# A hybrid decoder layer: four edits to where sums land, when loads are issued and how the order of the work is reckoned

## The chip, the cores and the metric

The kernel runs on one core of a Trainium2 chip. The metric is the device time of the whole program in microseconds (us), the median of several executions. The engines are called PE (TensorE), DVE (VectorE), ACT (ScalarE), POOL (GpSimd) and SP (SyncE, which here only issues transfers).

## The reference

One decoder layer in float32 on x of 1024 positions by 1024 channels. Cut to what is computed:

```python
h = rms_norm(x, ln_pre_mix)
proj = h @ w_in                      # 256 pooling channels, then q, k, v of 12 heads of 64
u, q, k, v = split(proj)
pool = multi_scale_pool(u, ...)      # 4 groups of 64: trailing means over 2/4/8/16 positions,
                                     # minus the token, a 64x64 map, a scale per channel
for window, dilation in ((128, 1), (512, 4), (2048, 16)):
    o, lse = dilated_branch(rope(q), rope(k), v, window, dilation)
o = sum(softmax(lse over the three) * o)
mixed = concat(pool, o)
x1 = x + rms_norm(mixed @ w_out, ln_post_mix)
g = rms_norm(x1, ln_pre_ffn)
f = (silu(g @ w_gate) * (g @ w_up)) @ w_down       # D_FF = 2816
out = x1 + rms_norm(f, ln_post_ffn)
```

## The kernel before, in words

**Numbers.** Every float32 operand of a large product is split into two float32r parts, a rounded one (hi, a cast on ACT) and what is left (lo, a subtraction on DVE or POOL). A product is three passes over them: hi by hi, hi by lo, lo by hi. `split` (L147 to 152) does both halves for a weight tile `wraw`; `wtile` loads and splits one. Channels lie on partitions, positions on the free axis, in two halves h of 512 positions.

**Attention stage (to about 410 us).** There are twelve units, a pair of heads p and a half h each. A unit has `scores` (products into banks `ps_s`, the mask and running minimum on DVE at L528, the exponential on ACT at L531), `merge` (the softmax joining: small DVE sums `ex`, a small PE product `ps_o<-ex,ls`, at L545), `weigh` (the probabilities `pp` multiplied by `wv` on POOL and DVE, L581) and `values` (turns of `pp` into `ps_t`, then products with v). Each step has a position in `plan`, a number given in the table `PRM`; `emit` sorts the steps by position and writes the program in that order. PE keeps program order; on DVE, ACT, POOL and SP a scheduler sets the order from modelled times.

The input projection's products (`ps_pj`) are the Fill between the steps. Besides having positions of their own, they are pulled by a reckoned clock: `clock` grows with every step written (0.235 per Fill product, 0.47 per score step), `due[key]` says at which reckoned time a result should be there, and `await_(key)` writes Fill products until the clock has come to it, at most 12 at a time. Table entries that matter below: `ls` (what follows a score step), `lw` (the weights of the joining), `f0` (where a unit's Fill starts), `first` (positions of unit 0), `cm` (splits of the mixed features).

**Pooling** is in unit 0 to 1: `pool_proj` makes `uf` and its split `u` (L692 to L695), `pool_means` multiplies u by band matrices (`ps_o<-band,u`), `pool_product` maps (`ps_o<-dhl,wp`).

**Output projection.** `mixed` loads the mixed features back (`mraw`) and splits them (`m`, L860/L861). `out_proj(h)` runs eight output tiles d; tile d's weights come by `weights(d)`, which is called at the middle of tile d-1, into `wraw` (two buffers). For h=1, tiles d=3 and d=5 have a split tile of their own, the others share `whl`. `chain(h)` is the norm after it, the residual sum with a second load of x (`xr`), the store `x1d` and the norm before the feed-forward part.

**Feed-forward.** The first two f tiles are plain products (`gate_up`). Then come ten groups j, in which a 2 by 2 block product is done with seven products P1 to P7 (`seven`), each as two rows i of 12 matmuls. `taken` and `gated` add the seven up on DVE: P1 is kept in `q` and `sq`, P7 in `sq` and `p`, and P5's bank `ps_s` is added to P7's. `down_sums` makes block sums of the down weights on POOL beside it. The last stage, from 988 us, is the down product, again by seven products; `operands` casts them on ACT and takes their lo parts on POOL (L1343) and DVE (L1344). The weights of the first group's seven (`rw`, L1193) are loaded and cast early, by `ahead`.

Nearly all transfers are issued by SP, in its order; one that has to wait for a buffer holds up those behind it.

Of the kernel before, what the change touches and what calls it, by code (L numbers as in the profile page):

```python
# [15 lines left out]
P = 128  # L16
# [54 lines left out]

# [36 lines left out]
def hybrid_block(ctx: ExitStack, tc: tile.TileContext, xT, w_in, w_pin, w_pool, w_out, w_gate, w_up, w_down,  # L108
# [28 lines left out]

    def raw_tile(src):
        r = wpool.tile([P, 1024], F32, name="wraw", tag="wraw", bufs=2)
        if len(src.ap) == 2:  # L140
            nc.sync.dma_start(r, src)
            return r
        r = r[:, :src.shape[1] * P]
        nc.sync.dma_start(r.rearrange("p (k m) -> p k m", m=P), src)
        return r
# [7 lines left out]

    def wtile(src, eng=None, pool=None, tag="whl", bufs=2):
        r = raw_tile(src)
        w = (pool or wpool).tile([P, 2, 1024], F32R, name=tag, tag=tag, bufs=bufs)
        split(w[:, :, :r.shape[-1]], r, eng or nc.gpsimd)
        return w
# [195 lines left out]
    def need(key, n):  # L354
        assert seen.get(key, 0) >= n, (key, n, seen.get(key, 0))
# [64 lines left out]
    G = PRM  # L420
# [64 lines left out]
    def scores(pr, h):  # L485
# [5 lines left out]
        def step(hd, side, jj):  # L491
# [26 lines left out]
            clock[0] += 0.47  # L518
            due["s", 0], due["s", 1] = due.get(("s", 1), 0.0), clock[0] + G["ls"]
            for j in (2 * jj, 2 * jj + 1):  # L520
                nb = 1 if narrow(side, h, j) else 2
                lo = 256 - nb * P
                so = s[:, (j % 2) * 256:(j % 2) * 256 + nb * P]
                row, mask = pt[:, j, lo:], (mB if side else mA)[:, lo:]
                if side == 0:
                    so = by_class(so)
                    row, mask = (x.rearrange("p (r c) -> p r c", c=4) for x in (row, mask))
                nc.vector.tensor_tensor_reduce(  # L528
                    row, so, mask, op0=ALU.add, op1=ALU.min, scale=-0.125,
                    scalar=3e38, accum_out=sx[:, 0, side, j, hd, 0:1])  # L530
                nc.scalar.activation(pt[:, j, lo:], pt[:, j, lo:], AF.Exp,  # L531
                                     bias=sx[:, 0, side, j, hd, 0:1], scale=-1.0,
                                     accum_out=sx[:, 0, side, j, hd, 1:2])
        return [lambda a=a: step(*a) for a in [(hd, sd, jj) for hd in range(2) for sd in (1, 0) for jj in range(2)]]

    def merge(pr, h):

        need(("s", pr.p, h), 8)
        un = pr.un[h]
        sx = un.sx  # L540
# [137 lines left out]
    def pool_proj(tt, k, n):  # L678
# [7 lines left out]
        if k == NK - 1 and n == 2:  # L686
# [7 lines left out]
            nc.scalar.activation(hi, f, AF.Copy)  # L694
            nc.gpsimd.tensor_tensor(lo, f, hi.bitcast(F32), ALU.subtract)  # L695

    def pool_bands():
# [6 lines left out]
    def pool_means(i, h):  # L704

        did(("means", i, h))
        d = pool.w["d", i, h] = att.tile([P, 2, 512], F32R, name="dhl", tag="ptr", bufs=PTB)
        sl = slice(i * P, (i + 1) * P)
# [124 lines left out]
    for u in range(1, 11):  # L833
        put(Fill([x for f in fill[u] for x in f]).by(3), u + G["f0"], u + (0.25 if u == 10 else 1) + G["f1"])
    put(Fill([x for h in range(2) for x in v_half(pairs[0], h)]).by(3), 0.0, G["pw"])
# [11 lines left out]
    def mixed(h, raw):  # L847
# [10 lines left out]
        def cut(n, sl):  # L858
            m[h][n] = room(h, n)
            nc.scalar.activation(m[h][n][:, sl, 0], got[n], AF.Copy)  # L860
            nc.vector.tensor_tensor(m[h][n][:, sl, 1], got[n], m[h][n][:, sl, 0].bitcast(F32), ALU.subtract)  # L861
        ids = [(n, slice(0, 1 if n == 2 else 2)) for n in (0, 1, 3, 2)]
# [22 lines left out]
    def out_proj(h, parts, done):  # L885
# [3 lines left out]
        def weights(d):  # L889
            if d not in box:  # L890
                box[d] = wtile(w_out[d], nc.gpsimd if d < 2 else nc.vector,
                               *((xgp, "xk5", 1) if d == 2 else (ffnl, "b%d" % (4 + d // 4), 1) if h and d in (3, 5) else ()))

# [34 lines left out]
    lm, cm = mixed(0, raws((0, 1)))  # L928
    put(lm, G["lm"], G["lm"])
    for step, at in zip(cm + [near], G["cm"]):  # L930
        put([step], at, 0)
    st, weights = out_proj(0, 3, None)
    put([lambda f=weights: f(0)], G["lm"], 0)
    put([lambda f=weights: f(1)], G["cm"][2], 0)
# [72 lines left out]
    def chain(h, sq, s3, at):  # L1007
# [4 lines left out]
        def load():  # L1012
            for n in range(2):
                x.append(slot((6, 4)[h] + n, [P, 4, 512], F32, "xr%d" % n))
                nc.sync.dma_start(x[n], xT[:, 4 * n:4 * n + 4, sl])

# [43 lines left out]

    emit((out_proj(1, 3, sqs[1][0].add)[0], 0.0, 1.0), *chain(0, *sqs[0], G["c0"]))

# [97 lines left out]
    def seven(j, order, rooms=()):  # L1160
# [66 lines left out]
        def taken(p, i):  # L1227
# [13 lines left out]
            elif p != "P5" or ("P7", i) in t:  # L1241
                own = [t[{"P4": "P1", "P5": "P7", "P3": "P6"}[p], n] for n in range(i + 1)]

                sum_to = own[i] if p == "P5" else ps
                nc.vector.tensor_tensor(sum_to, own[i], ps, ALU.add)
# [26 lines left out]
    one, ahead = seven(EARLY // 2, ("P1", "P2", "P6", "P5", "P7", "P4", "P3"), (6, 7))  # L1272
    ahead = ahead()
    ws += [{0: ftile(w_gate[f], f), 1: ftile(w_up[f], f)} for f in range(1, EARLY)]
# [271 lines left out]
```

## Time and profile before

| | |
|---|---|
| runs | 1214.27, 1218.79, 1220.18 us; median 1218.79 |
| profiled execution | 1218.72 us, of which the span is 1216.9 |
| PE busy | 1160.3 us, 95% of the span |
| DVE, POOL, ACT busy | 805.2 (66%), 596.3 (49%), 541.1 (44%) |
| transfers | 158.6 MB, mean 130 GB/s |
| PE idle from 561 to 984 us | none to speak of |

A busy time is the union of an engine's instructions. A number in brackets behind a row of the timeline is idle time of that engine just before, with the instruction that the profile names as its end. The column of PE's clock is the granted share of full speed: 1.00 is 2.4 GHz, and 0.50 would be 1.2 GHz, so 0.86 over a stretch of 25 us means that 7 us of it (0.14 / 0.5 x 25) were at the lower level.

### The profile page before, as it was taken

Reading aid. Unit: us, or ns where it says so; the run is one execution under the profiler, and the core shown is the slowest. Engines: PE = TensorE matmul, PEld = TensorE weight load, DVE = VectorE, ACT = ScalarE, POOL = GpSimd, SP = SyncE. Lnnn points to the kernel's source line nnn. Section 1 sums busy time; section 2 is a strip of 40 time slices with the busy share of each in tenths; the row PEclk is TensorE's granted clock in tenths of the full one; section 3 lists DMA queues with packets and bytes.
Section 4 is the critical chain, followed back from the end, with each engine's and each line's share of the span. In section 5 each row is a group of like instructions: output and inputs, shape, how many; then the busy total and the mean of one; then the engine's idle time right before and its main releaser. Section 6 shows DMA issues by size and latency. Waiting matters only on the chain.

```text
span 1216.9 us, 16713 instructions
## 1 busy us (share of the span) xinstructions
PE 1160.3 (95%) x5942; PEld 980.2 (81%) x5942; DVE 805.2 (66%) x1465; ACT 541.1 (44%) x1021; POOL 596.3 (49%) x533
## 2 busy tenths in 40 slices
PE   8999999999999898899999999999999989999996
PEld 6888888878887787777888888888888868888896
DVE  7935967686868756667965756566565584454585
ACT  6455655553656665475532232223321435343430
POOL 0131536364345222232176787577765967656521
PEclk9998999999999899999999999999999999999998
DMA  7101101011101312842034443554444849666642
GB/s 267 56 22 53 44 27 44 27 32 38 44 27 53 105 70 87 287 146 96 18 142 187 156 180 140 185 196 165 156 158 169 280 161 383 215 208 190 191 138 70
DMA packets 68435, 158.60 MB, mean 130 GB/s; under 512 B 8064, under 2 KB 11392, under 8 KB 66944
## 3 DMA queue, kind: packets, MB, share of 16 engines
q1 hardware_dynamic: 67776, 157.01, 37.1%
q8 instruction: 47, 0.77, 0.3%
q10 hardware_dynamic: 576, 0.52, 0.1%
q14 instruction: 36, 0.29, 0.1%
HBM read 114.51 MB, written 42.99 MB: 129 GB/s over the span
## 4 chain that ended last, share of the span: by engine, by line
PE 78%; DVE 13%; issue 3%; POOL 2%; DMA 2%; ACT 2%; SPq 0%; DVEq 0%; POOLq 0%; ACTq 0%
PE ps_pj L113 28%; PE ps_o L113 21%; PE ps_s L113 20%; PE ps_t L113 6%; PE ps_t L116 3%; DVE pp L528 1%; DVE sq L1209 1%; DMA mraw<-mixd 1%; DVE ql L344 1%; DVE k L337 1%; DVE rsw L312 1%; DVE ptr L622 1%; DVE whl L152 1%; DVE b L1022 1%; DVE v L478 1%
## 5 line engine op out<-in xcount | busy, mean ns | idle before, releaser
L113 PE MATMUL ps_pj<-x,whl 128*128 128x512 f32 x720 | 215.8, 421 | 1.5 <-ACT whl L148 0.9
L113 PEld LDWEIGHTS ps_pj<-x,whl 128*128 128x128 f32 x720 | 131.4, 193 | 19.6 <-ACT whl L148 1.1
L1203 POOL TENSOR_TENSOR fw<-rw,fw 128x512 fp32r<-128x512 f32 x74 | 106.3, 1460 | 61.5 <-ACT fw L1201 61.4
L581 POOL TENSOR_SCALAR pp<-pp,wv 128x256 f32<-128x256 f32 (+1 forms) x156 | 72.6, 484 | 95.8 <-DVE wv L565 91.9
L113 PE MATMUL ps_o<-tT,fw 128*128 128x512 f32 x504 | 117.8, 390 | 0.0
L531 ACT ACTIVATE pp<-pp,sx 128x128 f32<-128x128 f32 (+1 forms) x192 | 89.5, 467 | 54.7 <-DVE sx L528 54.1
L113 PEld LDWEIGHTS ps_o<-tT,fw 128*128 128x128 f32 x504 | 94.6, 188 | 20.0
L1203 POOL TENSOR_TENSOR whl<-rw,whl 128x512 fp32r<-128x512 f32 x42 | 61.5, 1488 | 58.6 <-ACT whl L1201 58.6
L314 POOL TENSOR_TENSOR rsw<-rsw,sinr 128x512 f32<-128x512 f32 x20 | 26.2, 1308 | 116.4 <-DVE rsw L312 116.4
L1201 ACT ACTIVATE fw<-rw 128x1024 fp32r<-128x1024 f32 x37 | 38.5, 1056 | 95.9 <-DVE rw L1169 40.9
L1343 POOL TENSOR_TENSOR op<-rw,op 128x512 fp32r<-128x512 f32 x38 | 60.7, 1596 | 39.3 <-ACT op L1342 37.3
L152 POOL TENSOR_TENSOR whl<-wraw,whl 128x512 fp32r<-128x512 f32 x34 | 46.0, 1374 | 59.4 <-ACT whl L148 59.4
L1342 ACT ACTIVATE op<-rw 128x1024 fp32r<-128x1024 f32 x38 | 40.3, 1061 | 64.6 <-PE ps_t L113 34.2
L622 DVE TENSOR_TENSOR ptr<-ps_t,ptr 128x512 fp32r<-128x512 f32 (+1 forms) x84 | 56.0, 668 | 16.5 <-ACT ptr L621 15.8
L621 ACT ACTIVATE ptr<-ps_t 128x512 fp32r<-128x512 f32 (+1 forms) x84 | 48.3, 576 | 41.6 <-PE ps_t L116 37.5
L113 PE MATMUL ps_pj<-b,fw 128*128 128x512 f32 x264 | 62.3, 392 | 0.0
L113 PE MATMUL ps_o<-ptr,v 128*128 128x128 f32 (+1 forms) x472 | 58.6, 259 | 3.8 <-DVE ptr L622 3.8
L113 PE MATMUL ps_s<-k,qh 128*128 128x128 f32 (+1 forms) x192 | 54.7, 296 | 6.4 <-DVE sx L528 6.3
L113 PEld LDWEIGHTS ps_o<-ptr,v 128*128 128x128 f32 x472 | 52.8, 165 | 7.4 <-DVE ptr L622 4.4
L113 PEld LDWEIGHTS ps_pj<-b,fw 128*128 128x128 f32 x264 | 49.6, 188 | 10.9
L113 PEld LDWEIGHTS ps_s<-k,qh 128*128 128x128 f32 x192 | 48.8, 254 | 11.7 <-DVE sx L528 8.4
L113 PE MATMUL ps_o<-tT,whl 128*128 128x512 f32 x216 | 52.3, 397 | 0.0
(302 smaller groups left out, 2898.6 us busy)
## 6 DMA issues: line engine op xcount, KB each, us to landing
rw<-bd SPq DMA_DIRECT2D x77, 256.0 KB, 4.6
rw<-wsd SPq DMA_DIRECT2D x44, 256.0 KB, 3.9
rw<-in_w_gate_dram SPq DMA_DIRECT2D x20, 512.0 KB, 3.6
rw<-in_w_up_dram SPq DMA_DIRECT2D x20, 512.0 KB, 4.6
wraw<-in_w_in_dram SPq DMA_DIRECT2D x17, 512.0 KB, 3.5
bd<-p SPq DMA_DIRECT2D x33, 256.0 KB, 2.9
rw<-in_w_down_dram SPq DMA_DIRECT2D x33, 256.0 KB, 4.9
wraw<-in_w_out_dram SPq DMA_DIRECT2D x16, 512.0 KB, 3.9
```

The lines of the kernel that those rows point to most:

```text
L113: return tc.keep_in_program_order(nc.tensor.matmul(*a, **k))
L116: return tc.keep_in_program_order(nc.tensor.transpose(dst, src, by))
L152: eng.tensor_tensor(dst[:, 1, at:at + w], src[:, at:at + w], dst[:, 0, at:at + w].bitcast(F32), ALU.subtract)
L314: eng[0].tensor_tensor(s, s, sinr[:, sl], ALU.mult)
L531: nc.scalar.activation(pt[:, j, lo:], pt[:, j, lo:], AF.Exp, bias=sx[:, 0, side, j, hd, 0:1], scale=-1.0, accum_out=sx[:, 0, side, j, hd, ...
L581: nc.gpsimd.tensor_scalar(pv, pv, un.wv[:, side, j, hd:hd + 1], 1.0, op0=ALU.mult, op1=ALU.mult)
L621: nc.scalar.activation(ptr[:, 0, :w], t[:, :w], AF.Copy)
L622: nc.vector.tensor_tensor(ptr[:, 1, :w], t[:, :w], ptr[:, 0, :w].bitcast(F32), ALU.subtract)
L1201: nc.scalar.activation(w[n][:, :, 0], raw[n], AF.Copy)
L1203: low[0] = nc.gpsimd.tensor_tensor(w[n][:, i, 1], raw[n][:, i], w[n][:, i, 0].bitcast(F32), ALU.subtract)
L1342: nc.scalar.activation(w[:, :, 0], raw, AF.Copy)
L1343: nc.gpsimd.tensor_tensor(w[:, 0, 1], raw[:, 0], w[:, 0, 0].bitcast(F32), ALU.subtract)
```

## The change

(a) **Fifth product.** P5's sums, which went back into `sq` and `p`, go to a bank of `ps_t`; what follows them (the factor r, the gating) reads them there.

(b) **Loads.** In `out_proj(1)`, tile d=3 gets a raw tile of its own (`b5`) and is loaded by an early `weights(3)`; d=5 goes back to the shared `whl`. The second half's `xr` and the first group's `rw` are issued behind the load of d=6 (`loads[-2]`).

(c) **Unit 0 and 1.** Unit 1's Fill starts at -0.07, unit 0's scores at 0.52, `ls` is 2.2, and `pool_means` awaits the reckoned time of its `u`.

(d) **Joining.** `merge` awaits 2.8 of reckoned time behind the unit's last score step.

(e) **Mixed features.** The lo splits go row by row (128x512), those of h=0, n<2 on POOL, at positions further apart.

```diff
-        'ls': 1.6,
+        'ls': 2.2,
+        'lm': 2.8,
...
-        'first': {'s0': 0.49, 's1': 0.64, ...},
+        'first': {'s0': 0.52, 's1': 0.64, ...},
...
-        'lm': 10.1,
-        'cm': (10.25, 10.27, 10.29, 10.33, 11.05),
+        'lr': 10.1,
+        'cm': (10.25, 10.3, 10.36, 10.42, 11.05),
...
-    def raw_tile(src):
-        r = wpool.tile([P, 1024], F32, name="wraw", tag="wraw", bufs=2)
+    loads = []
+
+    def raw_tile(src, own=None):
+        r = own or wpool.tile([P, 1024], F32, name="wraw", tag="wraw", bufs=2)
         if len(src.ap) == 2:
-            nc.sync.dma_start(r, src)
+            loads.append(nc.sync.dma_start(r, src))
...
             due["s", 0], due["s", 1] = due.get(("s", 1), 0.0), clock[0] + G["ls"]
+            due["m", pr.p, h] = clock[0] + G["lm"]
...
     def merge(pr, h):
 
         need(("s", pr.p, h), 8)
+        await_(("m", pr.p, h))
...
             nc.gpsimd.tensor_tensor(lo, f, hi.bitcast(F32), ALU.subtract)
+            due["u", h] = clock[0] + 3.2
...
         did(("means", i, h))
+        await_(("u", h))
...
-        put(Fill([x for f in fill[u] for x in f]).by(3), u + G["f0"], ...)
+        put(Fill([x for f in fill[u] for x in f]).by(3), u + (G["f0"] if u > 1 else -0.07), ...)
...
-            nc.vector.tensor_tensor(m[h][n][:, sl, 1], got[n], m[h][n][:, sl, 0].bitcast(F32), ALU.subtract)
+            for i in range(sl.start, sl.stop):
+                (nc.gpsimd if h == 0 and n < 2 else nc.vector).tensor_tensor(
+                    m[h][n][:, i, 1], got[n][:, i - sl.start], m[h][n][:, i, 0].bitcast(F32), ALU.subtract)
...
             if d not in box:
+                own = h == 1 and d == 3
                 box[d] = wtile(w_out[d], nc.gpsimd if d < 2 else nc.vector,
-                               *((xgp, "xk5", 1) if d == 2 else (ffnl, "b%d" % (4 + d // 4), 1) if h and d in (3, 5) else ()))
+                               *((xgp, "xk5", 1) if d == 2 else (ffnl, "b4", 1) if own else ()),
+                               raw=big(5, [P, 1024], F32, "b5") if own else None)
...
-                nc.sync.dma_start(x[n], xT[:, 4 * n:4 * n + 4, sl])
+                with tc.issue_after(behind.ins) if h else ExitStack():
+                    nc.sync.dma_start(x[n], xT[:, 4 * n:4 * n + 4, sl])
...
-    emit((out_proj(1, 3, sqs[1][0].add)[0], 0.0, 1.0), *chain(0, *sqs[0], G["c0"]))
+    st, weights = out_proj(1, 3, sqs[1][0].add)
+    weights(3)
+    emit((st, 0.0, 1.0), *chain(0, *sqs[0], G["c0"]))
+    behind = loads[-2]
...
-                sum_to = own[i] if p == "P5" else ps
+                sum_to = bank("t") if p == "P5" else ps
...
-    ahead = ahead()
+    with tc.issue_after(behind.ins):
+        ahead = ahead()
```

**Where the order moves, first place: DVE at the last group of the seven products.** `ps_...` are PSUM banks, `sq`, `p`, `q`, `r` lie in SBUF. Before:

```order
L1212 TENSOR_TENSOR rb<-rb,ps_pj 128x512
L1238 TENSOR_TENSOR sq<-ps_o,q 128x512
L1238 TENSOR_TENSOR p<-ps_o,sq 128x512
L1245 TENSOR_TENSOR sq<-sq,ps_s 128x512
L1209 TENSOR_TENSOR sq<-sq,r_5125 128x512
L1245 TENSOR_TENSOR p<-p,ps_s 128x512
L1212 TENSOR_TENSOR p<-sq,p 128x512
```

With the change:

```order
L1227 TENSOR_TENSOR rb<-rb,ps_pj 128x512
L1253 TENSOR_TENSOR sq<-ps_o,q 128x512
L1253 TENSOR_TENSOR p<-ps_o,sq 128x512
L1261 TENSOR_TENSOR ps_t<-sq,ps_s 128x512
L1224 TENSOR_TENSOR sq<-ps_t,r_5131 128x512
L1261 TENSOR_TENSOR ps_t<-p,ps_s 128x512
L1227 TENSOR_TENSOR p<-sq,ps_t 128x512
```

The order is the same; two instructions that read two SBUF tiles (`sq<-sq,r` and `p<-sq,p`) now read one SBUF tile and one bank.

**Second place: SP's transfers at `out_proj(1)`**, from the load of tile d=2 on. `xr` is x read again, `rw` the first group's gate and up weights, `b` the raw tile of d=3. Before (the weights of d=5 to 7 follow behind the `x1d`):

```order
L144 DMA wraw<-in_w_out_dram 128x1024 x2
L1015 DMA xr_5548<-in_xT_dram 128x4x512
L1015 DMA xr_5128<-in_xT_dram 128x4x512
L1015 DMA xr_5126<-in_xT_dram 128x4x512
L1193 DMA rw<-in_w_gate_dram 128x1024
L1193 DMA rw<-in_w_up_dram 128x1024
L1193 DMA rw<-in_w_gate_dram 128x1024
L1193 DMA rw<-in_w_up_dram 128x1024
L144 DMA wraw<-in_w_out_dram 128x1024 x2
L1023 DMA x1d<-z_4586 128x512
L1015 DMA xr_5550<-in_xT_dram 128x4x512
L1023 DMA x1d<-z_4586 128x512 x3
```

With the change (one more `rw` and the second half's two `xr` follow):

```order
L147 DMA wraw<-in_w_out_dram 128x1024 x2
L1027 DMA xr_5139<-in_xT_dram 128x4x512
L1027 DMA xr_5137<-in_xT_dram 128x4x512
L147 DMA b_5132<-in_w_out_dram 128x1024
L147 DMA wraw<-in_w_out_dram 128x1024 x2
L1035 DMA x1d<-z_4589 128x512 x4
L1035 DMA x1d<-z_4590 128x512 x4
L147 DMA wraw<-in_w_out_dram 128x1024
L1208 DMA rw<-in_w_gate_dram 128x1024
L1208 DMA rw<-in_w_up_dram 128x1024
L147 DMA wraw<-in_w_out_dram 128x1024
L1208 DMA rw<-in_w_gate_dram 128x1024
```

The weights of d=3, 4 and 5 now follow the first half's `xr` at once; both `xr` of the second half and all `rw` now come behind the stores `x1d` and the load of d=6.

**Third place: PE at the third pooling mean.** `ps_pj<-x,whl` are pooling projections, `ps_pj<-whl,x` is the Fill. Before:

```order
L113 MATMUL ps_pj<-whl,x_118 128x256 x3
L113 MATMUL ps_o<-dhl,wp 128x512 x3
L113 MATMUL ps_pj<-whl,x_119 128x256 x3
L113 MATMUL ps_pj<-whl,x_120 128x256 x3
L113 MATMUL ps_o<-band,u_694 128x144
L113 MATMUL ps_o<-band,u_695 128x144
```

With the change:

```order
L114 MATMUL ps_o<-dhl,wp 128x512 x3
L114 MATMUL ps_pj<-whl,x_119 128x256 x3
L114 MATMUL ps_pj<-whl,x_120 128x256 x3
L114 MATMUL ps_pj<-x_113,whl 128x512 x3
L114 MATMUL ps_pj<-x_114,whl 128x512 x3
L114 MATMUL ps_pj<-x_115,whl 128x512 x3
L114 MATMUL ps_pj<-x_116,whl 128x512 x3
L114 MATMUL ps_pj<-x_117,whl 128x512 x2
L114 MATMUL ps_o<-band,u_676 128x144
L114 MATMUL ps_o<-band,u_677 128x144
```

Fourteen products of unit 1's k projection now stand between the last pooling projection and the mean that needs its `u`.

## Rows read from the trace of the kernel before

**Rows 1.** The page's busy times: us (share), instructions.
```profile
PE 1160.3 (95%) x5942; PEld 980.2 (81%) x5942; DVE 805.2 (66%) x1465; ACT 541.1 (44%) x1021; POOL 596.3 (49%) x533
```

**Rows 2.** Stretches: length, busy us (count) PE PEld DVE ACT POOL, PEclk, DMA, GB/s.
```profile
50.00:75.00 25.00, 22.48 (x149) 21.56 (x148) 13.65 (x48) 13.01 (x45) 4.40 (x5) 0.86 0.01 3
75.00:100.00 25.00, 21.88 (x143) 20.24 (x142) 8.99 (x24) 10.71 (x21) 10.82 (x18) 0.86 0.20 67
...
175.00:200.00 25.00, 23.35 (x142) 20.85 (x141) 18.84 (x59) 14.00 (x42) 13.03 (x19) 0.93 0.03 12
...
500.00:525.00 25.00, 21.18 (x84) 16.53 (x83) 21.51 (x26) 16.38 (x26) 6.72 (x5) 0.86 0.83 302
975.00:1000.00 25.00, 20.02 (x82) 15.79 (x81) 19.65 (x17) 7.93 (x9) 17.34 (x15) 0.93 0.39 128
```

**Rows 3.** PE's waits by what ended them: us in total, times, longest.
```profile
PE ps_s L113 <- DVE sx L528: 6.3, 9, 1.2
PE ps_o L113 <- DVE ex L545: 6.1, 4, 1.6
```

**Rows 4.** Timeline of the last group: start, us, engine, line, operation, [idle before].
```profile
969.26 14.53 DVE L1209 TENSOR_TENSOR sq<-sq,r 128x512 f32<-128x512 f32 x1
969.49 1.31 POOL L1344 TENSOR_TENSOR fw<-rw,fw 128x512 fp32r<-128x512 f32 x1
...
976.50 2.96 PE L113 MATMUL ps_s<-b,whl 128*128 128x512 f32 x12
...
981.98 1.25 POOL L1344 TENSOR_TENSOR op<-rw,op 128x512 fp32r<-128x512 f32 x1
...
984.44 4.35 PE L113 MATMUL ps_s<-b,whl 128*128 128x512 f32 x12 [4.98 <-DVE p L1245]
```

**Rows 5.** DVE operations by line: count, ns min/median/max, first and last start.
```profile
L1245 DVE TENSOR_TENSOR sq<-sq,ps_s x10: 673/683/689, 621.6 to 968.5; 128x512 f32<-128x512 f32 x10
...
L1209 DVE TENSOR_TENSOR sq<-sq,r x10: 691/694/14526, 622.3 to 969.3; 128x512 f32<-128x512 f32 x10
...
L1344 DVE TENSOR_TENSOR fw<-rw,fw x22: 673/694/1794, 1004.5 to 1174.5; 128x512 fp32r<-128x512 f32 x22
```

**Rows 6.** Timeline at the start of the down product: an operand, and its first use.
```profile
1002.20 1.45 DVE L1344 TENSOR_TENSOR op<-rw,op 128x512 fp32r<-128x512 f32 x2
...
1018.89 0.86 PE L113 MATMUL ps_pj<-op 128*128 128x512 f32 x3
```

**Rows 7.** Timeline of the second output projection, tiles d=3 and 4.
```profile
514.89 7.55 PE L113 MATMUL ps_s<-fw,b 128*128 128x512 f32 x22 [3.82 <-DVE b L152]
...
520.40 1.06 ACT L1201 ACTIVATE op<-rw 128x1024 fp32r<-128x1024 f32 x1
...
522.28 5.77 PE L113 MATMUL ps_pj<-fw,whl 128*128 128x512 f32 x24
...
528.93 1.21 DVE L152 TENSOR_TENSOR whl<-wraw,whl 128x1024 fp32r<-128x1024 f32 x1
529.06 1.20 PE L113 MATMUL ps_s<-fw,b 128*128 128x512 f32 x4 [0.54 <-DVE b L152]
```

**Rows 8.** Timeline of units 0 and 1.
```profile
58.84 0.47 PE L113 MATMUL ps_s<-k,qh 128*128 128x128 f32 x1 [1.23 <-DVE sx L528]
...
88.17 2.53 POOL L152 TENSOR_TENSOR whl<-wraw,whl 128x512 fp32r<-128x512 f32 x2 [1.66 <-ACT whl L148]
...
90.93 0.33 PE L113 MATMUL ps_o<-band,u 128*128 128x128 f32 x1 [1.19 <-ACT u L694]
...
92.47 2.49 PE L113 MATMUL ps_o<-band,u 128*128 128x128 f32 x13 [1.21 <-POOL u L695]
```

**Rows 9.** Timeline of two joinings: PE behind DVE, and PE behind POOL.
```profile
184.17 0.43 PE L113 MATMUL ps_o<-ex,ls 128*128 128x64 f32 x2 [1.48 <-DVE ex L545]
...
392.94 0.75 PE L116 MATMUL ps_t<-idt,pp 128*128 128x128 f32 x4 [0.52 <-POOL pp L581]
```

**Rows 10.** Timeline: the last attention unit's turn, behind the mixed features' splits.
```profile
407.94 0.87 PE L116 MATMUL ps_t<-pmt,pp 128*128 128x128 f32 x3 [3.34 <-DVE v L478]
```

More of the change, by code (lines that the diff above doesn't have):

```diff
@@ L136, in cload @@
         return t
-    def raw_tile(src):
-        r = wpool.tile([P, 1024], F32, name="wraw", tag="wraw", bufs=2)
+    loads = []
+    def raw_tile(src, own=None):
+        r = own or wpool.tile([P, 1024], F32, name="wraw", tag="wraw", bufs=2)
         if len(src.ap) == 2:
-            nc.sync.dma_start(r, src)
+            loads.append(nc.sync.dma_start(r, src))
             return r
         r = r[:, :src.shape[1] * P]
-        nc.sync.dma_start(r.rearrange("p (k m) -> p k m", m=P), src)
+        loads.append(nc.sync.dma_start(r.rearrange("p (k m) -> p k m", m=P), src))
         return r
@@ L152, in split, with wtile @@
             eng.tensor_tensor(dst[:, 1, at:at + w], src[:, at:at + w], dst[:, 0, at:at + w].bitcast(F32), ALU.subtract)
-    def wtile(src, eng=None, pool=None, tag="whl", bufs=2):
-        r = raw_tile(src)
+    def wtile(src, eng=None, pool=None, tag="whl", bufs=2, raw=None):
+        r = raw_tile(src, raw)
         w = (pool or wpool).tile([P, 2, 1024], F32R, name=tag, tag=tag, bufs=bufs)
@@ L833, in hybrid_block @@
     for u in range(1, 11):
-        put(Fill([x for f in fill[u] for x in f]).by(3), u + G["f0"], u + (0.25 if u == 10 else 1) + G["f1"])
+        put(Fill([x for f in fill[u] for x in f]).by(3), u + (G["f0"] if u > 1 else -0.07), u + (0.25 if u == 10 else 1) + G["f1"])
     put(Fill([x for h in range(2) for x in v_half(pairs[0], h)]).by(3), 0.0, G["pw"])
@@ L928, in hybrid_block @@
     lm, cm = mixed(0, raws((0, 1)))
-    put(lm, G["lm"], G["lm"])
+    put(lm, G["lr"], G["lr"])
     for step, at in zip(cm + [near], G["cm"]):
@@ L932, in hybrid_block @@
     st, weights = out_proj(0, 3, None)
-    put([lambda f=weights: f(0)], G["lm"], 0)
+    put([lambda f=weights: f(0)], G["lr"], 0)
     put([lambda f=weights: f(1)], G["cm"][2], 0)
@@ L1242, in taken @@
                 own = [t[{"P4": "P1", "P5": "P7", "P3": "P6"}[p], n] for n in range(i + 1)]
-                sum_to = own[i] if p == "P5" else ps
+                sum_to = bank("t") if p == "P5" else ps
+                t["sum", i] = sum_to
                 nc.vector.tensor_tensor(sum_to, own[i], ps, ALU.add)
```

2 rows, old and new, of the table PRM are left out of this document.

## The prediction, made blind

> **What bounds the kernel now.** I read the page's busy times first: PE is busy for 95% of the span [rows 1], so with 1216.9 us less 1160.3 there are 57 us in which it does nothing. The change takes no matmul away; it can win only idle time of PE, or time in which PE ran at the lower clock. So I next read the stretches of 25 us, where the reader is to see four kinds of place with PE below 25 us and a granted clock below 1.00: units 0 and 1, a joining, the second output projection, the end of the seven products [rows 2]. There each idle piece is followed by work at the lower level. Then PE's waits by what ended them say which are many and small (`sx`, `ex`) [rows 3], and the timeline shows the single large ones [rows 4, 7, 8, 10]. About 0.5% (6 us) is what a measurement of this kernel can tell from no change. The sum below is made against the profiled execution's 1218.72 us (1216.9 of span and 1.8 around it); the median of the runs, 1218.79, is the same within 0.1, so nothing is corrected.
>
> **(a) The fifth product.** In the last of ten groups DVE's `sq<-sq,r` takes 14.53 us [rows 4]; its median over the ten is 0.694 [rows 5]. While it lasts, POOL runs its lo parts one behind the other, the first at 969.49 and the last at 981.98 to 983.23, about eleven of 1.25 to 1.31 us [rows 4]. The instruction ends when POOL pauses. Behind it on DVE stands `p<-p,ps_s`, which frees the bank that PE's next product wants: PE waits 4.98 us and then needs 4.35 us for twelve products that took 2.96 just before, 1.39 more at the lower clock [rows 4]. Both go if the stall goes: 6.4 us. Does it? With the change the instruction reads a bank and one SBUF tile. The one beside it that already did so, `sq<-sq,ps_s`, took at most 0.689 us in ten groups [rows 5]. I take the whole 6.4; the ends are 0 (the stall stays) and 6.4. The change adds no instruction here, and the seven products leave the banks of `ps_t` unused. The gain lasts to the end of the program: the tightest operand I found in the down product is ready at 1003.65 and first used at 1018.89 [rows 6], so all can come 6 us earlier.
>
> The trace shows a DVE instruction with two SBUF inputs held up for as long as eleven POOL instructions follow one another [rows 4], and those with a bank among their inputs never held up [rows 5]. The Trainium skill, "SBUF — State Buffer", "Who interferes with whom", says that a DVE instruction with two SBUF inputs contends with a GpSimd instruction that reads SBUF and one with at most one SBUF input does not; on this the rows agree. It also says that whoever issues first has the shared port pair for the whole instruction, which by the letter would be one instruction's wait, not eleven; that is a rival below.
>
> **(b) Loads of the second output projection.** Tile d=3's weights are late: PE waits 3.82 us for their split, and 22 products then take 7.55 us, where 24 of the next tile take 5.77 [rows 7], which is 5.29 for 22, so 2.26 lost to the clock. Tile d=5 waits 0.54 more [rows 7]. Together 6.6, the most there is to win. Before d=3's load SP issues three `xr` of 1 MB and four `rw` of 0.5 MB, 5 MB; with the change two `xr` are left. At the stretch's 302 GB/s [rows 2] that is 3 MB, 10 us, less, far over 3.82; so the wait goes. What is late next: the moved loads. The casts `op<-rw`, at 517 and 520.40 before [rows 7], stay ahead of d=5's copy on ACT, and their `rw` now queue behind `x1d` and d=6: 2.5 to 3 MB from about 515 at that rate is 10 us, 525. ACT stands until then, and with it the copies that free PE's banks; PE would then be some 14 us into d=3 to 5 and have two banks in turn, so I deduct 2 us. The split of d=6 and 7 now needs `whl` back from d=4 and 5; a cast of 1.06 and a split of 1.21 fit beside a tile's 5.77 [rows 7] and cost nothing, unless ACT is stuck, which is in the 2. I take 5; the ends are -3 (ACT holds PE for a full 10 us, against 6.6 won) and 6.6. `xr` of the second half is used only after the tiles are done, some 20 us later.
>
> **(c) Units 0 and 1.** Waits of 1.23 for `sx`, and of 1.19 and 1.21 for `u` [rows 8]: 3.6 us. Both stretches have 0.86 [rows 2], that is 7 us at half speed in each, of which (b) showed 2.26 lost per such stretch. If all goes: 3.6 + 2 x 2.26 = 8.1, and at most 3.5 us per stretch, 10.6. The fourteen products put before the third pooling mean cover it: each is about 0.24 us of PE's work (5.77/24 [rows 7]), 3.4 us against 2.4 waited. They come from Fill that stood elsewhere, and they need `whl`, which POOL has split only at 88.17 + 2.53 = 90.70 [rows 8], 0.3 to 1.6 us behind where PE would want it. So 8.1 less about 1.6, rounded: 6, with ends 1 (only a wait replaced by another) and 10.
>
> **(d) Joining.** PE waits 6.1 us in four joinings for `ex` [rows 3], 1.48 at 184.17 [rows 9], where the stretch has 0.93, 3.5 us at the lower level, at most 1.75 lost [rows 2]. In odd units some nine Fill products instead of seven now stand between the scores and the joining, 0.5 us more cover for 1.5 of wait. They leave gaps later in the unit, so I take half: 3. The ends are -3 (two of the units get a new wait of 1.5) and 8 (6.1 and 1.75). The rest of the waits on `sx` (6.3 less 1.23 [rows 3]) I leave as they are: the Fill that would cover them is the same.
>
> **(e) Mixed features.** One turn waits 3.34 us for `v` [rows 10], because DVE stands behind splits whose casts wait for the transfer `mraw`. ACT's casts stay where they were, so most of it stays. Two smaller splits per cast let DVE go on a little earlier: 0.6, about one 128x512 operation of 0.69 [rows 5]. POOL's four new ones of 1.3 [rows 4] lie between weighings: ends -1 and 4.
>
> **Sum**: 6.4 + 5 + 6 + 3 + 0.6 = 21.0, so 1218.7 - 21.0 = **1197.7 us**. All upper ends together (35) would give 1183, all lower ones (-6) 1225; neither is likely to come at once.
>
> **The rivals.**
> *The attention's gaps only move* (18%). For it: Fill is a fixed stock, PE products unchanged, and each product put before one wait is missing at another. Against: the two largest gaps of (c) are followed by Fill that could have stood before them. Then (c), (d), (e) give nothing: 1218.7 - 11.4 = 1207.3.
> *DVE's stall stays* (10%). If one instruction of POOL were all that DVE can lose, 1.3 us [rows 4], as the 1.79 at most of DVE's two-SBUF-input operations in the last stage suggests (1.1 over the median, beside the same POOL work) [rows 5], then 12 of the 14.5 us have another cause, and the bank changes nothing: 1197.7 + 6.4 = 1204.1. That is the Trainium skill's rule of one whole instruction, named above. Against: ten of ten neighbours with a bank took 0.69.
> *The moved loads hold PE* (7%). The gate weights or `rw` come late and ACT stands: (b) turns from +5 to -8, PE waiting where it did not, 1197.7 + 13 = 1210.7. For it: 2.5 MB behind `x1d`; against: two banks of slack and 20 us to the first use.
> *Only (a) works* (7%), the reckoned clock being a model and the loads only exchanged: 1218.7 - 6.4 = 1212.3, the edge of no change.
> *Slower* (5%). The joining now comes later in each of twelve units, the weighing on POOL starts later by as much, and PE's turns, which wait for `pp`, find the Fill used up. PE does wait for POOL's `pp` already, 0.52 at 392.94 [rows 9]. A new wait of 1.5 us, the size at 184.17 [rows 9], with 1.75 at the lower clock [rows 2] in each unit is 39 us, against 18.0 won by (a), (b), (c), (e): 1218.7 + 39 - 18 = 1239.7. It decides from six units on (6 x 3.25 = 19.5). Against it: in the order of the changed program the turns are still written behind the same weighings with Fill between.
>
> **How the numbers follow.** The forecast has what is left, 53%. Faster by over 0.5% (below 1212.7): forecast, the first three rivals but for a tail of 2 in 100, and half of *only (a)*: 0.86. Within 0.5%: the other half and tails of the loads and the gaps, 0.09. Slower: 0.05. The range of 8 in 10 goes from 1187 (three quarters of the way from the sum to all its upper ends) to 1212, which takes in all rivals but the slower one and half of *only (a)*.
>
> **What would show it.** Right: DVE's product with r in the last group at about 0.69 us and no wait of PE near 984; the clock at 1.00 in that stretch; no wait of PE for d=3's split near 515; the clock of 50 to 100 us at 0.93 or above and the waits for `u` gone; waits for `ex` down from 6.1 to about 3; the wait at 408 still there. Wrong: the 14.5 us on another operation of DVE with PE behind it; ACT idle for `rw` near 520 with PE behind its copies; waits of PE for `pp` or `ptr` in many units.

## The result, and the profile after

The changed kernel takes 1205.06 us (median of 4 runs, 1203.25 to 1207.24) against 1218.56 (4 runs, 1214.27 to 1220.18): ratio 0.9895, 95% interval 0.9865 to 0.9926, 13.5 us faster. The forecast was 1197.7 in a range of 1187 to 1212: the direction and the range held, but a third of the 21.0 us did not come. The profiled execution took 1204.66 us, 14.1 less than that of before; its span is 1202.8.

Where the gain arises is read from the start of the same PE instruction in the two timelines (us; units counted from 0):

| PE's step | before | after | ahead by |
|---|---|---|---|
| last pooling mean | 102.00 | 95.73 | 6.3 |
| joining of unit 3 | 182.31 | 172.58 | 9.7 |
| joining of unit 9 | 382.71 | 377.09 | 5.6 |
| joining of unit 10 | 423.54 | 418.50 | 5.0 |
| second output projection, d=3 | 510.33 | 505.55 | 4.8 |
| first gate product | 546.86 | 540.82 | 6.0 |
| first product P6 | 605.95 | 598.46 | 7.5 |
| down product | 988.63 | 974.60 | 14.0 |

So 9.7 us are won by unit 3 and about half is lost again by unit 10; 2.7 come at the output projection and after it (4.8 to 7.5), and 6.5 in the last group. The rows are of one execution each. Three runs below, e1, e6 and e12, have the changed kernel's order of instructions on PE, DVE, ACT and POOL up to 614 us, and they reach the first product P6 at 597.07, 595.96 and 598.83; so a difference of up to 3 us between two profiles need not be the effect of an edit. The pattern is the same in all four: 4.7 to 7.6 us lost from unit 3 to unit 10, and in the other three 3.8 won from the output projection to P6.

The stretches of the changed kernel, columns as in [rows 2]:

```profile
50.00:75.00 25.00, 23.88 (x183) 23.32 (x183) 16.68 (x57) 15.84 (x50) 4.59 (x6) 1.00 0.02 4
75.00:100.00 25.00, 24.13 (x157) 22.66 (x156) 9.41 (x24) 12.52 (x26) 10.08 (x17) 0.93 0.25 77
...
400.00:425.00 25.00, 20.98 (x114) 18.32 (x114) 16.33 (x45) 11.59 (x31) 5.93 (x9) 0.83 0.15 43
500.00:525.00 25.00, 25.00 (x110) 20.21 (x109) 24.11 (x34) 20.43 (x33) 5.05 (x3) 1.00 0.74 278
525.00:550.00 25.00, 22.31 (x96) 18.20 (x95) 13.64 (x13) 14.03 (x24) 15.97 (x12) 0.86 0.29 101
...
975.00:1000.00 25.00, 25.00 (x111) 20.55 (x111) 18.03 (x14) 7.49 (x8) 16.96 (x13) 1.00 0.63 222
```

The low clock of 50 to 75, of 500 to 525 and of 975 to 1000 is gone; that of the output projection has moved to 525 to 550, and 400 to 425 is at 0.83 (0.86 before). PE's waits (us in total, times, longest), to be held against [rows 3]:

```profile
PE ps_o L114 <- DVE ex L550: 5.1, 5, 1.4
PE ps_o L114 <- DVE ptr L627: 4.9, 3, 2.6
PE ps_t L117 <- DVE v L481: 4.2, 4, 2.5
PE ps_t L117 <- DVE ptr L627: 4.0, 1, 4.0
PE ps_s L114 <- DVE sx L532: 3.4, 3, 2.0
PE ps_o L114 <- DVE sq L999: 2.7, 1, 2.7
```

`ex` and `sx` have fallen from 6.1 and 6.3. The wait of 4.98 for `p` is gone; new is one of 2.7 for `sq`, and the one for `ptr` ahead of a turn (`ps_t`) is 4.0, where it was 1.02. The timeline at the places of [rows 7, 8, 10]:

```profile
85.75 3.42 PE L114 MATMUL ps_pj<-x,whl 128*128 128x512 f32 x14
89.01 2.29 PE L114 MATMUL ps_o<-band,u 128*128 128x144 f32 x20
...
398.42 0.82 PE L117 MATMUL ps_t<-pmt,pp 128*128 128x128 f32 x3 [2.51 <-DVE v L481]
402.45 2.96 POOL L155 TENSOR_TENSOR whl<-wraw,whl 128x512 fp32r<-128x512 f32 x2 [2.24 <-ACT whl L151]
402.93 3.63 DVE L869 TENSOR_TENSOR m<-mraw,m 128x512 fp32r<-128x512 f32 x3
407.16 0.55 DVE L627 TENSOR_TENSOR ptr<-ps_t,ptr 128x384 fp32r<-128x384 f32 x1
407.76 1.13 PE L117 MATMUL ps_t<-idt,vT 128*128 128x128 f32 x4 [4.02 <-DVE ptr L627]
...
505.55 5.76 PE L114 MATMUL ps_s<-fw,b 128*128 128x512 f32 x24
518.75 2.02 ACT L1216 ACTIVATE op<-rw 128x1024 fp32r<-128x1024 f32 x2
532.04 1.83 PE L114 MATMUL ps_o<-ones,sq 128*128 128x1 f32 x8 [2.69 <-DVE sq L999]
```

The fourteen products run through and the mean behind them waits for nothing; d=3 starts without its 3.82 us and at full speed, and ACT casts `rw` without any idle time ahead. At 402.93 DVE does three row splits `m` in a row; `ptr`, which PE waits for, comes behind them. The turn behind `ptr` and the sum of squares in the kernel before:

```profile
414.69 0.75 PE L116 MATMUL ps_t<-idt,vT 128*128 128x128 f32 x4 [1.02 <-DVE ptr L622]
...
541.08 0.95 PE L113 MATMUL ps_o<-ones,sq 128*128 128x1 f32 x8
```

### The profile page after: what moved, and what is told of

Same layout as the page of the kernel before. It is cut to its first block, busy times and chain, and to the rows that moved or that the text cites. A ratio compares the mean times of both kernels' runs of the same rounds, so it can differ in the third digit from the quotient of the medians.

```text
span 1202.8 us, 16715 instructions
## 1 busy us (share of the span) xinstructions
PE 1156.9 (96%) x5942; PEld 982.1 (82%) x5942; DVE 793.6 (66%) x1467; ACT 541.1 (45%) x1021; POOL 595.6 (50%) x537
## 4 chain that ended last, share of the span: by engine, by line
PE 81%; DVE 10%; issue 3%; ACT 3%; DMA 2%; POOL 1%; SPq 0%; DVEq 0%; ACTq 0%; POOLq 0%
PE ps_pj L114 29%; PE ps_o L114 22%; PE ps_s L114 20%; PE ps_t L114 7%; PE ps_t L117 3%; DVE pp L532 1%; DVE whl L155 1%; DVE ptr L627 1%; DMA wraw<-in_w_out_dram 1%; DVE sq L999 1%; DMA mraw<-mixd 1%; DMA xraw<-in_xT_dram 0%; DVE k L340 0%; DVE rsw L315 0%; DVE v L481 0%
## 5 line engine op out<-in xcount | busy, mean ns | idle before, releaser
L1218 POOL TENSOR_TENSOR fw<-rw,fw 128x512 fp32r<-128x512 f32 x74 | 101.8, 1401 | 65.4 <-ACT fw L1216 65.4
```

The source lines that it names most:

```text
L1218: low[0] = nc.gpsimd.tensor_tensor(w[n][:, i, 1], raw[n][:, i], w[n][:, i, 0].bitcast(F32), ALU.subtract)
```

## The experiments

Eleven kernels were run in twelve runs (e12 is e1 again), in groups of four, four, two and two; each time stands against the kernel before in its own group (medians 1219.13, 1218.13, 1218.22 and 1218.74).

| run | what | us | ratio to before, interval |
|---|---|---|---|
| e1 | (a) undone | 1211.94 | 0.9931 (0.9903 to 0.9958) |
| e12 | the same | 1212.64 | 0.9952 (0.9930 to 0.9973) |
| e6 | the same, POOL idle there | 1204.41 | 0.9890 (0.9854 to 0.9927) |
| e2 | (b) undone | 1208.70 | 0.9915 (0.9900 to 0.9930) |
| e5 | (c) undone | 1213.06 | 0.9948 (0.9927 to 0.9969) |
| e3 | (d) undone | 1201.99 | 0.9857 (0.9842 to 0.9872) |
| e4 | (e) undone | 1200.81 | 0.9844 (0.9824 to 0.9865) |
| e7 | (d), (e) undone | 1200.33 | 0.9842 (0.9813 to 0.9871) |
| e8 | e7, means later | 1197.66 | 0.9827 (0.9799 to 0.9854) |
| e9 | e8, `ex` on POOL | 1202.53 | 0.9866 (0.9827 to 0.9906) |
| e10 | e8 with (e), more rows on POOL | 1196.25 | 0.9827 (0.9792 to 0.9862) |
| e11 | e10, `ex` on POOL in three units | 1194.82 | 0.9802 (0.9780 to 0.9824) |

**The fifth product: e1, e12, e6.**

```diff
-                sum_to = bank("t") if p == "P5" else ps
+                sum_to = own[i] if p == "P5" else ps
```

> The changed kernel with (a) undone: P5's sums go back to `sq` and `p`. Theory (DVE held up by a run of POOL instructions when both its inputs are in SBUF): the long `sq<-sq,r` of the last group is back with 10 us or more, PE waits some 5 us behind it, and the time is 1205.1 + 6.5 = 1211.6 us; nothing changes ahead of 960 us. Rival (another cause, the bank does nothing): no long instruction, 1205 us.

The median rises by 6.9 us, as the theory has it. But the six times run from 1203.45 to 1215.5, and the profiled execution was the one of 1203.45: no long `sq<-sq,r`, and no wait of PE behind it. So the same kernel was run again.

> The kernel of the first run again ((a) undone), to catch an execution with the stall in the profile. Theory: where the time is above 1208 the profile has `sq<-sq,r` or another two-SBUF-input instruction of that chain at 5 us or more beside an unbroken run of POOL, and PE waits behind it near 970; where the time is near 1204 it has not. Rival: a time above 1208 without such an instruction, the difference lying elsewhere.

Its profiled execution took 1212.0 us, 8.5 more than that of e1. Of these, 1.8 are there at P6 (598.83 against 597.07), and 6.7 come at the last group. The timelines of the two executions, e1 first:

```profile
960.38 0.70 DVE L1224 TENSOR_TENSOR sq<-sq,r 128x512 f32<-128x512 f32 x1
960.48 1.76 POOL L1361 TENSOR_TENSOR fw<-rw,fw 128x512 fp32r<-128x512 f32 x1
...
968.00 1.05 DVE L1227 TENSOR_TENSOR p<-sq,p 128x512 f32<-128x512 f32 x1 [4.94 <-ACT sq L1225]
968.46 1.75 POOL L1361 TENSOR_TENSOR fw<-rw,fw 128x512 fp32r<-128x512 f32 x1
```

and e12:

```profile
961.73 1.33 POOL L1361 TENSOR_TENSOR fw<-rw,fw 128x512 fp32r<-128x512 f32 x1
962.14 13.97 DVE L1224 TENSOR_TENSOR sq<-sq,r 128x512 f32<-128x512 f32 x1
...
974.25 1.31 POOL L1361 TENSOR_TENSOR op<-rw,op 128x512 fp32r<-128x512 f32 x1
976.76 5.10 PE L114 MATMUL ps_s<-b,whl 128*128 128x512 f32 x12 [4.42 <-DVE p L1261]
```

In e1 DVE began 0.1 us ahead of POOL's instruction: DVE took 0.70, and POOL's took 1.76 instead of some 1.3. In e12 DVE began 0.4 us behind one, and ended at 976.11, 0.55 us behind the end of POOL's run (975.56). The Trainium skill, "SBUF — State Buffer", "Who interferes with whom", has it that whoever issues first keeps the shared port pair for the whole instruction; the two first rows agree, and so does the row at 968.00, where DVE is held for some 0.4 us within one POOL instruction. The 13.97 us agree only if POOL's next instruction takes the pair each time ahead of the waiting DVE, which that section doesn't state. Why DVE got in at 968.00 and not at 962.14 stays open. To see whether POOL is the cause, its run was taken away:

```diff
-        nc.gpsimd.tensor_tensor(w[:, 0, 1], raw[:, 0], ...)
-        (nc.gpsimd if p == "P1" else nc.vector).tensor_tensor(w[:, 1, 1], raw[:, 1], ...)
+        (nc.vector if p == "P1" else nc.gpsimd).tensor_tensor(w[:, 0, 1], raw[:, 0], ...)
+        nc.vector.tensor_tensor(w[:, 1, 1], raw[:, 1], ...)
```

> The changed kernel with (a) undone as in the first run, and in the down product the lo parts of P1's operands taken on DVE instead of POOL, so that POOL's run beside the last group is thinned out; P1 being what is cast first there. Theory (the run of POOL instructions holds DVE's two-SBUF-input instruction): no DVE instruction of the last group over 3 us in the profile, and the times lie within 4 us of one another like those of the changed kernel, at 1205, instead of 1203 to 1215 as with (a) undone alone. Rival (the long instruction has another cause): times spread over some 10 us again, median near 1212. DVE's added work may cost up to 2 us in either.

```profile
960.00:970.00 10.00, 10.00 (x45) 8.20 (x44) 8.94 (x16) 4.65 (x5) 0.00 (x0) 1.00 0.71 232
```

POOL is idle from 960 to 970, `sq<-sq,r` takes 0.68 us, and three of four runs lie within 1203.23 and 1204.69. The fourth took 1211.26, so the times do not lie within 4 us of one another as the theory had it, and no profile shows what happened in it. These times do not settle the cause by themselves, since e1's profile had no long `sq<-sq,r` either. Another instruction of DVE with both inputs in SBUF does, `rw<-rw,q`, some 17 us later. In the changed kernel:

```profile
979.05 6.32 DVE L1356 TENSOR_TENSOR rw<-rw,q 128x512 f32<-128x512 f32 x1 [4.54 <-DMA q<-bd]
...
983.53 1.29 POOL L1360 TENSOR_TENSOR whl<-rw,whl 128x512 fp32r<-128x512 f32 x1
```

and in e6, without POOL's run:

```profile
979.55 0.69 DVE L1356 TENSOR_TENSOR rw<-rw,q 128x512 f32<-128x512 f32 x1 [2.31 <-DMA q<-bd]
```

In the changed kernel it ends at 985.37, again 0.55 us behind the end of POOL's run (984.82). In all eleven profiles in which POOL's run goes on there it takes 5.2 to 7.0 us. So POOL's run is the cause. It also follows that (a) does not end such stalls: it takes the one away that PE stood behind, and a shorter one comes later, behind which ACT waits for `rw` and PE does not (25.00 busy from 975 to 1000).

**The loads: e2, e8.** (b) undone:

```diff
-                own = h == 1 and d == 3
-                ... (ffnl, "b4", 1) if own else ()), raw=big(5, [P, 1024], F32, "b5") if own else None)
+                ... (ffnl, "b%d" % (4 + d // 4), 1) if h and d in (3, 5) else ()))
...
-    weights(3)
...
-    with tc.issue_after(behind.ins):
-        ahead = ahead()
+    ahead = ahead()
```

> The changed kernel with (b) undone. Theory (the wait for d=3 was won, but PE then comes earlier to the sum of squares at the end of the output projection, which had been covered): the wait for d=3 of some 3.8 us is back, the 2.7 us wait for `sq` near 532 is gone, and the time is 2.7 us more, 1207.8. Rival (the 2.7 us wait comes from elsewhere, from the splits that moved to other tiles or from DVE): it stays, and the time is 6 to 7 us more, 1211.5.

```profile
510.60 6.84 PE L114 MATMUL ps_s<-fw,b 128*128 128x512 f32 x22 [3.85 <-DVE b L155]
524.78 5.40 PE L114 MATMUL ps_s<-fw,b 128*128 128x512 f32 x22 [1.26 <-DVE b L155]
...
536.80 0.95 PE L114 MATMUL ps_o<-ones,sq 128*128 128x1 f32 x8
```

3.6 us more, nearer to the theory's 2.7 than to the rival's 6.5, and its sign is in the rows: the wait for d=3 is back, that for `sq` is gone. With (b) PE arrives at the sum of squares of the norm (`ps_o<-ones,sq`) before DVE has added the last square. e8 puts that step and its like in the second chain a little later; its base is e7, below:

```diff
-        'c0': (0.13, 0.2, 0.21, 0.6, 0.3, 0.7, 0.9, 0.99),
-        'c1': (0.08, 0.17, 0.18, ...),
+        'c0': (0.13, 0.2, 0.21, 0.6, 0.3, 0.7, 0.945, 0.998),
+        'c1': (0.11, 0.178, 0.18, ...),
```

> As the run before with (d) and (e) undone, and the two sums of squares of the second output projection put later (first chain 0.90 to 0.945 and its rows 0.99 to 0.998, second chain 0.08 to 0.11 and its rows 0.17 to 0.178). Theory (PE now comes to them before DVE has summed the squares, 2.2 to 2.7 us and 0.6 to 2.2 us): the two waits fall to 1.2 us and under 0.5, and the time is 2 to 3 us less than that run, 1195. Rival (PE only waits at the rows behind them instead, for `nrr`): the waits move there and the time is the same within 1 us.

```profile
528.03 1.02 PE L114 MATMUL ps_o<-ones,sq 128*128 128x1 f32 x8 [0.47 <-DVE sq L996]
...
532.69 0.65 PE L117 MATMUL ps_o<-idt,nrr 128*128 128x128 f32 x4 [1.19 <-POOL nrr L180]
```

1197.66 against 1200.33, 2.7 us: in e7's profile the two waits for `sq` were 2.39 and 1.04 us; one of 0.47 is left, and 1.19 for `nrr` is the part that moved, as the rival has it. The intervals overlap, so the time alone would not show it; the profiles do: from the start of d=3 to the first product P6 the four with the later step (e8 to e11) take 88.6 to 89.6 us, the seven others with (b) 91.8 to 93.5.

**Units 0 and 1: e5.**

```diff
-        'ls': 2.2,
+        'ls': 1.6,
...
-        'first': {'s0': 0.52, ...},
+        'first': {'s0': 0.49, ...},
...
-        await_(("u", h))
...
-        ... u + (G["f0"] if u > 1 else -0.07) ...
+        ... u + G["f0"] ...
```

> The changed kernel with (c) undone: unit 1's Fill and unit 0's scores where they were, `ls` at 1.6, no await ahead of the pooling means. Theory (all that was won up to unit 2 is (c)): the two waits for `u` and the one for `sx` in units 0 and 1 are back, unit 2's joining comes 8 to 9.6 us later, and, since (d) and (e) cost what they cost without it, the time is 1213 to 1214.7 us. Rival (Fill is only moved: what (c) wins at the start it takes from units 3 to 9): unit 2 is later by as much, but the gap closes again to 4 or 5 us by the end of the attention, 1209.5 us.

```profile
90.17 0.33 PE L114 MATMUL ps_o<-band,u 128*128 128x128 f32 x1 [1.19 <-ACT u L699]
91.70 2.46 PE L114 MATMUL ps_o<-band,u 128*128 128x128 f32 x13 [1.21 <-POOL u L700]
```

The waits for `u` are back to the hundredth of a microsecond, and the median is 8.0 us higher, 1213.06 (1208.46 to 1215.05; the profiled execution, 1215.05, was the longest). Its unit 3 joins at 181.53, 9.0 us behind the changed kernel, its unit 8 still 8.0 behind (349.44 against 341.48). So the gain of (c) is not taken back later and the rival falls; what was lost from unit 3 on points to (d) and (e), and e7 below bears that out.

**Joining and mixed features: e3, e4, e7.** e3 takes out one line, e4 puts the splits and positions of (e) back, e7 does both:

```diff
-        await_(("m", pr.p, h))
...
-        'cm': (10.25, 10.3, 10.36, 10.42, 11.05),
+        'cm': (10.25, 10.27, 10.29, 10.33, 11.05),
...
-            for i in range(sl.start, sl.stop):
-                (nc.gpsimd if h == 0 and n < 2 else nc.vector).tensor_tensor(m[h][n][:, i, 1], ...)
+            nc.vector.tensor_tensor(m[h][n][:, sl, 1], got[n], ...)
```

> The changed kernel without the await of (d) in `merge`. Theory (the wait in the joining is for `ex`, which stands on DVE behind the rope of the Fill that the await pulls in, so more Fill ahead covers nothing, and it is missing later): the waits for `ex` stay at 5 us within 1, and the attention from unit 3 on is 0 to 2.5 us shorter: 1202.6 to 1205. Rival (the await works, and what was lost from unit 3 on is Fill spent in units 0 and 1): waits for `ex` rise by 2 us or more and the time is 1207 to 1209.

```profile
PE ps_o L114 <- DVE ex L549: 7.5, 6, 1.7
...
PE ps_o L114 <- DVE ptr L626: 2.6, 3, 1.7
...
PE ps_s L114 <- DVE sx L532: 2.0, 3, 1.1
```

The time is 3.1 us less, which was the theory's sign, but the reason was only half right: without the await the waits for `ex` do rise, 5.1 to 7.5, as the rival said. What the await covers there it takes from `ptr` (4.9 with it, 2.6 without) and `sx` (3.4 and 2.0): Fill was moved from one wait to others. Where the 3.1 us arise the profile does not show: e3 comes to unit 11's joining at 450.79, the changed kernel at 450.34, and e1, e6 and e12, with the await, at 451.53 to 452.37.

> The changed kernel with (e) undone. Theory (the row splits stand together on DVE, 3.6 us, ahead of the split `ptr` that PE waits 4.0 us for): that wait falls to about 1.0 us, the one for `v` ahead of it goes from 2.5 back to 3.3, and the time is 2.2 us less, 1202.9. Rival (the 4.0 us come from the other parts, which bring PE there earlier): the wait stays above 3 us and the time is the same or 0.8 more, 1205 to 1206.

```profile
402.83 3.50 POOL L155 TENSOR_TENSOR whl<-wraw,whl 128x512 fp32r<-128x512 f32 x2 [12.16 <-ACT whl L151]
...
403.83 1.37 DVE L868 TENSOR_TENSOR m<-mraw,m 128x1024 fp32r<-128x1024 f32 x1
...
406.07 1.00 PE L117 MATMUL ps_t<-idt,vT 128*128 128x128 f32 x4 [1.69 <-DVE ptr L627]
```

4.3 us less, more than the 2.2 expected; the wait for `ptr` is 1.69 instead of 4.02, that for `v` 3.32 instead of 2.51, and unit 10's joining comes 2.1 us earlier (416.44 against 418.50). The rest of the 4.3 comes later and lies within what profiles of one order differ by. In the changed order the three row splits that are left to DVE stand together; they took 3.63 us for 3 x 0.69 of work, beside POOL's split of `whl`.

> The changed kernel with (d) and (e) both undone: (a), (b) and (c) alone. If the two losses are separate they add: 1205.1 less 3.1 and less 4.3, 1197.7 us. Rival (both are the same loss, the last unit's turn behind DVE, which can be won once): 1200 to 1201 us.

1200.33: the two losses don't add (the rival's 1200 to 1201). In its profile unit 3 joins at 173.53, 8.8 us ahead of the kernel before, and unit 11 at 447.53, still 7.8 ahead; in the changed kernel 9.7 had become 5.0. With (e) undone, taking (d) out changes nothing that can be measured (1200.81 and 1200.33).

**Versions that go further: e10, e9, e11.** e10 is without (d), with the later means, and gives POOL the third block's rows too:

```diff
-                (nc.gpsimd if h == 0 and n < 2 else nc.vector).tensor_tensor(
+                (nc.gpsimd if h == 0 and n != 2 else nc.vector).tensor_tensor(
```

> (a), (b), (c) and (e) without (d), with the later sums of squares, and of the mixed features' row splits also those of the third block on POOL, so that one of three is left on DVE ahead of `ptr`. Theory (the turn waits for `ptr` behind DVE's three row splits, 3.6 us): PE's wait there falls from 4 us to 2 or less, and the time is 1196 to 1198, the level of (a), (b), (c) alone with the later sums. Rival (PE waits for the transfer and the casts whoever splits): the wait stays above 3 us, 1199 to 1201.

```profile
401.69 1.45 DVE L868 TENSOR_TENSOR m<-mraw,m 128x512 fp32r<-128x512 f32 x1
...
404.35 1.13 PE L117 MATMUL ps_t<-idt,vT 128*128 128x128 f32 x4 [1.51 <-DVE ptr L626]
```

One split is left ahead of `ptr`, and PE waits 1.51 us: with the queue on DVE shortened, the wait goes. e9 and e11 try what is left at the joining:

```diff
-            nc.vector.tensor_tensor(ex[:, sd], ...)
+            (nc.gpsimd if sd else nc.vector).tensor_tensor(ex[:, sd], ...)
```

(e9, on the base of e8; e11, on that of e10, has `if sd and h and 0 < pr.p < 4`.)

> As the run with the later means ((a), (b), (c) and later sums of squares), and the second of the joining's two `ex` products taken on POOL instead of DVE. Theory (PE's wait for `ex` is DVE's queue: the instruction stands behind the rope of the Fill, while its input is ready): the waits for `ex`, 7.5 us in six joinings, fall to 4 us or less, and the time is 2 to 4 us less than 1197.7. Rival (the wait is for the last exponential on ACT, wherever `ex` is computed): they stay at 6 us or more, and the time is the same or, POOL's instructions of 1.3 us standing ahead of `ex`, up to 3 us more.

```profile
PE ps_t L117 <- POOL pp L585: 6.2, 2, 4.1
...
PE ps_o L114 <- POOL ex L549: 3.2, 4, 1.1
```

The waits for `ex` fall from 7.5 to 3.2 us, as the theory has it, yet the time is 4.9 us more: in unit 1 the weights `wv` now come behind a rope of the Fill on DVE, POOL's weighing is late, and PE waits 4.1 us for `pp`. A local gain, and a reordering elsewhere that costs more.

> As the run with the third block's rows on POOL, and the joining's second `ex` on POOL in the second-half units of pairs 1 to 3 alone, where PE waits 1.71, 1.71 and 1.36 + 1.24 us for DVE. Theory (DVE's queue is that wait, and the loss of the run with every `ex` on POOL came from unit 2, whose order changed): the waits there fall to 0.8 us each, no new wait over 2 us for `pp`, and the time is 1193 to 1196. Rival (any such move reorders the rest of DVE's and POOL's work): new waits take it back, 1196 to 1200.

1194.82 us, ratio 0.9802 (0.9780 to 0.9824): the fastest version tried, 10 us below the changed kernel and 24 below the one before. In its profile the waits at the joinings of units 3 and 5 are 0.80 instead of 1.71, but one of 2.64 for `ptr` near 262 has taken the place of 0.58; its interval overlaps that of e10, so this last step alone is not shown to help.

## Why the prediction was right or wrong, step by step

(a) Right: forecast 6.4, measured 6.9 and 7.6 by undoing it, 6.5 in the traces. The operand in a bank is what counts, and the gain did carry to the end. What the prediction could not see from one execution: the stall does not come in every execution of one program (e1 and e12). The ten times of the two run from 1203.45 to 1215.5; the 6.7 us of the stall are a part of that, and the rest is not explained: the times of e5, whose sums lie in a bank, spread by 6.6 us too. Its sign of being wrong, a long instruction of DVE elsewhere with PE behind it, came by half: `rw<-rw,q`, 6.32 us, without PE behind it. The rival by the rule of one whole instruction is wrong for the length of the wait (eleven instructions, e12; the long `rw<-rw,q` saw four to six) and right for another one in the same chain (e1 at 968.00).

(b) Mis-sized: forecast 5, measured 3.6. All that was to be won at d=3 was won. The deduction of 2 us was put on the wrong successor: "ACT stands until then". ACT cast `rw` at 518.75 without idle time. Late next was the sum of squares at the end of the projection, hidden before because PE itself came late; it took 2.69 us and moved the low clock to 525 to 550. The step that failed is the search for what is late next: it looked at the transfers that the change moves and not at the other engines' work that ends just ahead of a PE step.

(c) Mis-sized the other way: forecast 6, measured 8.0. The 1.6 us deducted for `whl`, split late on POOL, did not come (85.75: fourteen products in 3.42 us, no wait; the split began at 84.31, 3.9 us earlier than before), and about the 8.1 of waits and clock did. The prediction's 8.1 less 1.6 is 6.5, besides, not 6.

(d) Wrong: "I take half: 3", measured nothing by itself (e7 against e4) and -3.1 beside (e). That the Fill would "leave gaps later in the unit" was named and taken as half; the runs show that it is the whole. This is, for one part, the rival in which gaps only move.

(e) Wrong: forecast +0.6, measured -4.3. The wait that the edit aims at is 0.8 less in the changed kernel's profile (2.51 for 3.34), but 2.78, 3.81 and 5.03 in e1, e6 and e12, which have the same order there, so that it shrank is not shown. The step that failed counted the new instructions on POOL and not where the rest of DVE's would stand: the three row splits left to it, together ahead of `ptr`, a wait of 4.02 us (3.52 to 4.15 in e1, e6 and e12) that was 1.02 before.

The sum by undoing: 6.9 + 3.6 + 8.0 and -4.7 for (d) and (e) together (e7) give 13.8, against 13.5 measured. The 7.2 us that this sum lacks of the forecast's 21.0 are 8.3 at (d) and (e) and 1.4 at (b), less 2.5 more at (a) and (c). For (a), (b) and (c) alone 17.4 were forecast, and e7, which has just these, is 17.8 below the kernel before. That is closer than the working earns, since what is missing at (b) and what is over at (a) and (c) cancel; and the whole lies in the range because the range is 25 us wide, not because (d) and (e) were understood.

One slip is in the chances. Faster is said to take in half of *only (a)*, but 0.53, 0.18, 0.10 and 0.07 less 0.02 make its 0.86 without that half. With it faster would have 0.895, and within 0.5% would have 0.055 and not 0.09.

## What to carry to other kernels

A wait that is filled with work from a fixed stock is won only if that work stood where nothing waited; ask for each filler which wait it covered before. When a split of work is moved or cut up, look at the order of the engine that keeps the rest, down to the instruction that TensorE waits for. And when a wait goes, the next one is often not a thing that the change moved, but a sum or a norm on another engine that had been just in time.

## What the runs showed of the hardware

A DVE instruction with both inputs in SBUF, alone 0.69 us, took 13.97 us when it began 0.4 us after one of POOL's in an unbroken run, of which eleven were left, and 0.70 us when it began 0.1 us ahead of one, which then took 1.76 instead of 1.3. The same program showed both (e12 and e1). Where such an instruction was held by a run of POOL, it ended 0.54 to 0.56 us behind the run's last instruction, in all thirteen cases of the last group and of `rw<-rw,q` behind it. With a PSUM bank for one input, `sq<-ps_t,r` took 0.690 to 0.694 us in all ten groups of each of ten profiles, and the last of each stood beside an unbroken run of POOL. In the changed kernel:

```profile
L1224 DVE TENSOR_TENSOR sq<-ps_t,r x10: 691/692/693, 614.9 to 961.8; 128x512 f32<-128x512 f32 x10
```
